# A two-layer decoder trunk on one core: where the head's weights land, the order of the normalisation between the layers, and 7 weight with 5 landing buffers

## The chip, the core and the metric

The kernel runs on one core of a Trainium2 chip. The metric is the device time of one execution in microseconds (us), less is better; several runs are taken and their median is compared.

## What is computed

Two layers, a sequence of 256 tokens, 2048 features, all in float32. Each layer projects its input x into queries, keys, values and gates of two attention branches (12 heads of 128 each), runs a dilated sliding-window attention and a forgetting attention, projects both up, merges them with gates computed from x, projects once more, and normalises:

```python
def hybrid_layer(x, pos, w_in, b_forget, b_gate, w_up_a, w_up_b, w_out, ln_g, ln_b):
    h = jnp.einsum('bsd,dc->bsc', x, w_in)
...
    return layer_norm(alpha * x + y, ln_g, ln_b)

def layer_norm(x, g, b):
    x32 = x.astype(jnp.float32)
    mu = jnp.mean(x32, axis=-1, keepdims=True)
    var = jnp.mean(jnp.square(x32 - mu), axis=-1, keepdims=True)
    y = (x32 - mu) * lax.rsqrt(var + LN_EPS)
    return (y * g.astype(jnp.float32) + b.astype(jnp.float32)).astype(x.dtype)
```

Nearly all of the work is the products of x, and of what comes from it, with the weights: 357 MB of weights are read once.

## The kernel before, in words

**Two halves of a number.** Every operand of a product is kept as a high half (ACT's copy into the fp32r type) and a low half (source less high half, on DVE); `split` (L68 to L70) makes both. A product of a weight tile of 128 x 128 with x is one 512-column matmul, the weight's high half with both halves of x (L164), and one 256-column matmul, its low half with x's high half (L162).

**Pieces.** The weights come in 716 pieces. `Piece.prep` loads one into a landing buffer `raw` (L63 to L66, on SP's queue, 7 buffers) and splits it into a weight buffer `w` (L82, 6 buffers), from which `Piece.run` feeds PE. A large piece is 128 x 1024: eight k-tiles (128 rows) of one unit, a unit being 128 columns of one projection. When a unit is complete, `fold` adds the two halves of its PSUM tile: ACT copies one (`c`, L173) and DVE adds the other (`p`, L175).

**The first units of a layer.** The first four units (`SIDE`) of each layer don't run one after the other. Their pieces are interleaved, and PE goes by pairs of k-tiles through all four: such a pair of one unit is called a block below (two 512-column and two 256-column matmuls, 1536 columns), 32 blocks in all. So PE can begin when the first tile of x is there. In layer 0 these units are cut into five chunks each, of 2, 2, 4, 4 and 4 k-tiles (20 pieces); in layer 1 into two of eight (8 pieces). x lives in eight tiles of two k-tiles each, here x_81 to x_88 by the names of the program; in layer 0 they are loaded by `load_x` (L114 to L120) into idle slots of the pool `s2` (L59), between the pieces, and split. x_81's load goes out on SP's queue, x_82's on ACT's, the others on SP's. Eight matmuls on zeros (`keep_warm`, L136 to L140) run ahead of the first real one.

**Between the layers.** `ln_stats` (L533 to L553) gets the mean and the reciprocal deviation from the sums that PE made, spreads them over the partitions by PE (`pm`, `pa`), and subtracts the mean from the first tile (DVE) and from the second (POOL). `ln_next` (L568 to L591) then makes x_81 to x_88 again, tile by tile: a front (subtract the mean, L565; multiply, L562 or L566; the affine step and x's high half on ACT, L577 for the first two tiles, L579 and L584 for the others; for the first two tiles the affine step on DVE too, L582) and a back (x's low half, DVE L589). The main loop (L655 on) lists fronts and backs in the order front 0, back 0, front 1, front 2, back 1, front 3, back 2 and so on, holds each behind the one before by `tc.issue_after`, and calls `prep_to` for the pieces. The framework's scheduler decides the rest of each engine's order: where splits of pieces stand between these steps.

Of the kernel before, what the change touches and what calls it, by code (L numbers as in the profile page):

```python
# [42 lines left out]
def trunk(ctx: ExitStack, tc: tile.TileContext, xt, w_st, w_v, w_vf, w_up, w_o,  # L43
# [17 lines left out]


    def load_raw(ap, n):  # L63
        t = wp.tile([128, SLOT], F32, name="raw", tag="raw", bufs=7)
        nc.sync.dma_start(t[:, :n], ap)
        return t[:, :n]  # L66

# [4 lines left out]
    class Piece:  # L72


        def __init__(self, unit, ap, kts, w):
            self.unit, self.ap, self.kts, self.w = unit, ap, kts, w
            self.first = self.last = False

        def prep(self):
            n = len(self.kts) * self.w  # L80
            raw = load_raw(self.ap, n)
            t = wp.tile([128, 2 * W_PART + 64], F32R, name="w", tag="w", bufs=6)  # L82
            o = W_OFF if self.w == 128 else V_OFF
            self.t = t[:, o:o + 2 * W_PART].rearrange("p (a b) -> p a b", a=2)
            split(self.t[:, 0, :n], self.t[:, 1, :n], raw)
# [28 lines left out]
    def load_x(k0, n):  # L114
        for k in range(k0, k0 + n, 2):
            raw = slot("xraw")
            (nc.scalar if k == 2 else nc.sync).dma_start(raw, xt[:, k:k + 2, :])
            x = xs[k // 2]
            for i in ((slice(0, 1), slice(1, 2)) if k == 0 else (slice(0, 2),)):
                split(x[:, i, 0], x[:, i, 1], raw[:, i])  # L120
# [81 lines left out]
    def build_layer(l):  # L202
# [97 lines left out]
        def mixer_pair(br, p):  # L300
# [77 lines left out]
            if br == 0 and p == 0:  # L378
                us = [q_u[0], k_u[0], z_u[0], q_u[1], k_u[1], v_unit, z_u[1]]
                chunks = (2, 2, 4, 4, 4) if l == 0 else (8, 8)  # L380
                for u in us[:SIDE]:
                    u.cut(chunks)
            elif has_f:
                us = [v_unit] + q_u + k_u + z_u
            else:
                us = q_u + k_u + [v_unit] + z_u
# [146 lines left out]
        def ln_stats():  # L533
            pst = ln["pst"]
            mu, m, rs = (sm.tile([128, 2], F32, name=n, tag=n, bufs=2) for n in ("mu", "m", "rs"))
            nc.vector.tensor_scalar(mu, pst[:, 0], 1.0 / D, None, op0=ALU.mult)
            nc.scalar.activation(m, pst[:, 0], AF.Square, scale=1.0 / D)
            nc.vector.scalar_tensor_tensor(m, pst[:, 1], 1.0 / D, m, op0=ALU.mult, op1=ALU.subtract)
            pm = spread(mu, "pm")
            if not final:  # L540
                keep_warm(3)
            nc.scalar.activation(m, m, AF.Sqrt, bias=eps)
            nc.vector.reciprocal(rs, m)
            pa = spread(rs, "pa")
            if not final:
                keep_warm(6)
            ms = att.tile([128, S], F32, name="ms", tag="lnc", bufs=1)
            nc.scalar.activation(ms, pm, AF.Copy)
            for i in range(2):
                nc.vector.tensor_tensor(ln[0][:, i], ln[0][:, i], pm, op=ALU.subtract)  # L550
            for j2 in pooled:
                nc.gpsimd.tensor_tensor(ln[j2], ln[j2], both(ms), op=ALU.subtract)
            ln["pm"], ln["pa"] = pm, pa  # L553

        def affine(j2):
            return ([t[:, l * KT + 2 * j2 + i:l * KT + 2 * j2 + i + 1] for i in range(2)] for t in (lng, lnb))

        def centred(j2):
            r = ln[j2]
            if j2 == 0:  # L560
                for i in range(2):
                    ins = nc.vector.tensor_tensor(r[:, i], r[:, i], ln["pa"], op=ALU.mult)  # L562
                return ins
            if j2 not in pooled:
                nc.vector.tensor_tensor(r, r, both(ln["pm"]), op=ALU.subtract)  # L565
            return nc.vector.tensor_tensor(r, r, both(ln["pa"]), op=ALU.mult)  # L566

        def ln_next(j2, quick):  # L568

            r, x = ln[j2], xs[j2]  # L570
            g, b = affine(j2)

            def front():
                ins = centred(j2)
                for i in range(2):
                    if quick:
                        nc.scalar.activation(x[:, i, 0], r[:, i], AF.Identity, scale=g[i], bias=b[i])  # L577
                    else:
                        nc.scalar.activation(r[:, i], r[:, i], AF.Identity, scale=g[i], bias=b[i])  # L579
                if quick:  # L580
                    for i in range(2):
                        ins = nc.vector.tensor_scalar(r[:, i], r[:, i], g[i], b[i], op0=ALU.mult, op1=ALU.add)  # L582
                else:
                    nc.scalar.activation(x[:, :, 0], r, AF.Copy)  # L584
                return ins

            def back():
                for i in (range(2) if quick else (slice(0, 2),)):
                    ins = nc.vector.tensor_tensor(x[:, i, 1], r[:, i], x[:, i, 0].bitcast(F32), op=ALU.subtract)  # L589
                return ins  # L590
            return front, back  # L591

        def ln_last(j2):
            r = ln[j2]
# [62 lines left out]
    for g in order:  # L657
        done += len(g)
        n = number[id(g[0].unit)]
        if g[0].first and n in norms:  # L660

            stats, apply = norms[n]
            stats()
            stages = [apply(j2, j2 < 2) for j2 in range(KT // 2)]
            run = [stages[0][0], stages[0][1], stages[1][0]]
            for j2 in range(2, KT // 2):
                run += [stages[j2][0], stages[j2 - 1][1]]
            run.append(stages[-1][1])
            ins = None
            for i, f in enumerate(run):  # L670
                if i == 9:
                    with tc.issue_after(ins.ins):
                        prep_to(done + 2)
                if ins is None:
                    ins = f()
                else:
                    with tc.issue_after(ins.ins):
                        ins = f()
        prep_to(done + 4)
        for p in g:  # L680
            if p.first:
                for f in jobs.get(number[id(p.unit)], []):
                    f()
                if p.unit.before:
                    p.unit.before()
        if len(g) > 1:
            for i in range(0, len(g[0].kts), 2):
                for p in g:
                    for part in range(2):
                        p.run(i, part)  # L690
                        p.run(i + 1, part)
        else:

            for part in range(2):
                for i in range(len(g[0].kts)):
                    g[0].run(i, part)
        for p in g:
            if p.last and p.unit.after:
                p.unit.after()
# [87 lines left out]
```

## Time and profile before

| | us |
|---|---|
| runs | 1979.55, 1979.7, 1981.81 |
| median | 1979.7 |
| profiled execution | 1979.52 |
| its span in the trace | 1977.7 |

The profile is that of one execution. Times in it count from the start of the span. PE is TensorE, PEld its weight loads, DVE VectorE, ACT ScalarE, POOL GpSimd, SP the engine that issues most transfers; a name with q is an engine's queue. A row of a timeline groups like instructions that follow one another: start, length of the group, what it is, how many, and in brackets how long the engine had idled before it and for whom. The matmuls' ends are modelled, so the spacing of starts tells more than the lengths.

### The profile page before, as it was taken

The page shows a single profiled execution, that of the slowest core. Times are in us where ns is not written, and L with a number is a line of the kernel's source. Part 1 is how long each engine was busy: PE and PEld are TensorE (multiplying, and loading weights), DVE is VectorE, ACT ScalarE, POOL GpSimd, SP SyncE. Part 2 cuts the span into 40 slices and gives each one's busy share as a digit, 9 for nine tenths or more (in the row PEclk, how much of TensorE's full clock was granted, in tenths as well). Part 3 has the DMA queues.
Part 4 walks back from the last instruction along what each step waited for, and adds up shares of the span by engine and source line. Part 5 has one row for each costly group of instructions (what it writes and reads, how often), then busy time and mean ns, then how long its engine had stood idle before and what let it go on. Part 6 is the DMA issues. An engine that isn't in the chain of part 4 may idle for free.

```text
span 1977.7 us, 29731 instructions
## 1 busy us (share of the span) xinstructions
PE 1957.8 (99%) x11449; PEld 1727.2 (87%) x11449; DVE 1269.8 (64%) x1908; ACT 987.3 (50%) x1558; POOL 69.5 (4%) x64
## 2 busy tenths in 40 slices
PE   9999999999999999999999999999999999999997
PEld 7888888889888888888888888888898888888886
DVE  7666665555555555668787666655555555556686
ACT  6444444444544445555465444445454444445544
POOL 0000000001000000001100000000010000000022
PEclk9999999999999999999999999999999999999998
DMA  9655555666656556665555555556666665556651
GB/s 307 204 180 179 172 169 172 192 197 211 185 178 183 179 170 180 183 202 192 160 181 171 179 176 178 166 181 185 203 203 185 185 179 179 170 174 191 210 184 64
DMA packets 108630, 362.74 MB, mean 183 GB/s; under 512 B 12464, under 2 KB 15944, under 8 KB 108488
## 3 DMA queue, kind: packets, MB, share of 16 engines
q1 hardware_dynamic: 107320, 357.42, 58.5%
q0 software_dynamic: 1024, 3.17, 0.7%
q8 instruction: 89, 1.46, 0.3%
q14 instruction: 53, 0.43, 0.1%
q10 hardware_dynamic: 144, 0.26, 0.1%
HBM read 358.68 MB, written 2.12 MB: 182 GB/s over the span
## 4 chain that ended last, share of the span: by engine, by line
PE 98%; DVE 1%; DMA 0%; ACT 0%; issue 0%; DVEq 0%; ACTq 0%
PE mm L164 53%; PE mm L162 27%; PE mm L353 8%; PE mm L355 4%; PE ps_s L258 1%; PE po L287 1%; PE pt L278 1%; PE po L288 1%; PE ps_s L257 1%; PE mm L351 0%; PE mm L348 0%; PE mm L349 0%; DMA xraw<-xt 0%; DVE gated L566 0%; DMA raw<-w_st 0%
## 5 line engine op out<-in xcount | busy, mean ns | idle before, releaser
L70 DVE TENSOR_TENSOR w<-raw,w 128x1024 fp32r<-128x1024 f32 (+3 forms) x716 | 840.5, 1178 | 443.5 <-ACT w L69 442.1
L69 ACT ACTIVATE w<-raw 128x1024 fp32r<-128x1024 f32 (+3 forms) x716 | 717.9, 1004 | 455.5 <-issue 222.6
L164 PE MATMUL mm<-x,w 128*128 128x512 f32 x3328 | 851.2, 396 | 6.4 <-DVE x L589 3.1
L164 PEld LDWEIGHTS mm<-x,w 128*128 128x128 f32 x3328 | 594.3, 188 | 109.9 <-ACT x L577 2.7
L162 PEld LDWEIGHTS mm<-x,w 128*128 128x128 f32 x3328 | 454.0, 188 | 39.2 <-DVE w L70 1.4
L162 PE MATMUL mm<-x,w 128*128 128x256 f32 x3328 | 463.8, 279 | 0.0
L173 ACT ACTIVATE c<-mm 128x256 f32<-128x256 f32 x320 | 120.3, 384 | 456.2 <-PE mm L162 422.5
L175 DVE TENSOR_TENSOR p<-mm,c 128x256 f32<-128x256 f32 x252 | 106.8, 425 | 186.9 <-ACT c L173 186.4
L164 PE MATMUL mm<-gated,w 128*128 128x512 f32 x768 | 196.6, 391 | 0.0
L353 PE MATMUL mm<-w,x 128*128 128x512 f32 x704 | 176.7, 393 | 0.0
L164 PEld LDWEIGHTS mm<-gated,w 128*128 128x128 f32 x768 | 135.3, 188 | 21.1
L353 PEld LDWEIGHTS mm<-w,x 128*128 128x128 f32 x704 | 126.1, 188 | 22.7
L164 PE MATMUL mm<-merged,w 128*128 128x512 f32 x480 | 120.1, 392 | 0.0
L162 PEld LDWEIGHTS mm<-gated,w 128*128 128x128 f32 x768 | 108.3, 188 | 10.4
L162 PE MATMUL mm<-gated,w 128*128 128x256 f32 x768 | 111.2, 279 | 0.0
L355 PEld LDWEIGHTS mm<-w,x 128*128 128x128 f32 x704 | 94.7, 188 | 7.4
L164 PEld LDWEIGHTS mm<-merged,w 128*128 128x128 f32 x480 | 86.0, 188 | 15.5 <-DVE merged L70 0.5
L355 PE MATMUL mm<-w,x 128*128 128x256 f32 x704 | 96.5, 279 | 0.0
L162 PEld LDWEIGHTS mm<-merged,w 128*128 128x128 f32 x512 | 68.1, 188 | 4.8
L162 PE MATMUL mm<-merged,w 128*128 128x256 f32 x512 | 69.9, 279 | 0.0
L447 POOL TENSOR_TENSOR u<-x 128x512 f32<-128x512 f32 x16 | 31.7, 1982 | 603.9 <-DVE merged L70 242.4
L267 ACT ACTIVATE z<-z,s 128x128 f32<-128x128 f32 x96 | 42.3, 444 | 0.0
(128 smaller groups left out, 910.9 us busy)
## 6 DMA issues: line engine op xcount, KB each, us to landing
raw<-w_st SPq DMA_DIRECT2D x408, 512.0 KB, 3.9
raw<-w_up SPq DMA_DIRECT2D x128, 384.0 KB, 3.1
raw<-w_v SPq DMA_DIRECT2D x88, 512.0 KB, 4.4
raw<-w_o SPq DMA_DIRECT2D x64, 512.0 KB, 4.1
raw<-w_vf SPq DMA_DIRECT2D x8, 536.0 KB, 4.4
raw<-w_st SPq DMA_DIRECT2D x12, 256.0 KB, 5.6
nb<-cum POOLq DMA_DIRECT2D x12, 256.0 KB, 4.5
yt<-gated SPq DMA_DIRECT2D x8, 256.0 KB, 2.1
```

The lines of the kernel that those rows point to most:

```text
L69: nc.scalar.activation(hi, src, AF.Copy)
L70: nc.vector.tensor_tensor(lo, src, hi.bitcast(F32), op=ALU.subtract)
L162: nc.tensor.matmul(o, w[:, 1], a[:, 0], start=False, stop=last)
L164: nc.tensor.matmul(ps(), w[:, 0], a, start=first, stop=False)
L173: nc.scalar.activation(c, ps[:, S:], AF.Copy, scale=scale)
L175: nc.vector.tensor_tensor(dst, ps[:, :S], c, op=ALU.add)
L257: nc.tensor.matmul(ps[:, 0], q[:, :128], k[:, :128], start=True, stop=True)
L258: nc.tensor.matmul(ps[:, 1:3].rearrange("p a b -> p (a b)"), q[:, 128:], k, start=True, stop=True)
L267: nc.scalar.activation(z[:, sl], z[:, sl], AF.Exp, scale=-1.0, bias=s4[:, c:c + 1], accum_out=s4[:, 2 + c:3 + c])
L353: nc.tensor.matmul(o, xh, w, start=first, stop=False)
L355: nc.tensor.matmul(o[:, :NV], xl, w[:, 0], start=False, stop=last)
L447: nc.gpsimd.tensor_tensor(u, x[:, :, 0], x[:, :, 1], op=ALU.add)
```

## The change

- The landing buffers go from 7 to 5 and the weight buffers from 6 to 7.
- The 20 pieces of the first four units of layer 0 land in slots of `s2` (`wraw`) instead of `raw`. x_82 is loaded by SP's queue like the rest.
- In `ln_stats` between the layers, 12 warm matmuls are asked for behind `pa` instead of 6.
- In `ln_next`, the subtraction of the mean is a step of its own (`shift`); for the first two tiles DVE writes its affine result to a new slot `y`; before, it overwrote `r`, which ACT reads too.
- The order becomes front 0, back 0, front 1, shift 2, back 1, front 2, then for each tile shift, front and the back of the tile before. One piece is asked for ahead of the statistics; two more calls for pieces stand behind the steps of tiles 4 and 5, in place of one.

```diff
@@ -61,7 +61,7 @@
 
 
     def load_raw(ap, n):
-        t = wp.tile([128, SLOT], F32, name="raw", tag="raw", bufs=7)
+        t = wp.tile([128, SLOT], F32, name="raw", tag="raw", bufs=5)
         nc.sync.dma_start(t[:, :n], ap)
         return t[:, :n]
 
@@ -74,12 +74,16 @@
 
         def __init__(self, unit, ap, kts, w):
             self.unit, self.ap, self.kts, self.w = unit, ap, kts, w
-            self.first = self.last = False
+            self.first = self.last = self.head = False
 
         def prep(self):
             n = len(self.kts) * self.w
-            raw = load_raw(self.ap, n)
-            t = wp.tile([128, 2 * W_PART + 64], F32R, name="w", tag="w", bufs=6)
+            if self.head:
+                raw = slot("wraw", (128, 2 * S))[:, :n]
+                nc.sync.dma_start(raw, self.ap)
+            else:
+                raw = load_raw(self.ap, n)
+            t = wp.tile([128, 2 * W_PART + 64], F32R, name="w", tag="w", bufs=7)
             o = W_OFF if self.w == 128 else V_OFF
             self.t = t[:, o:o + 2 * W_PART].rearrange("p (a b) -> p a b", a=2)
             split(self.t[:, 0, :n], self.t[:, 1, :n], raw)
@@ -114,7 +118,7 @@
     def load_x(k0, n):
         for k in range(k0, k0 + n, 2):
             raw = slot("xraw")
-            (nc.scalar if k == 2 else nc.sync).dma_start(raw, xt[:, k:k + 2, :])
+            nc.sync.dma_start(raw, xt[:, k:k + 2, :])
             x = xs[k // 2]
             for i in ((slice(0, 1), slice(1, 2)) if k == 0 else (slice(0, 2),)):
                 split(x[:, i, 0], x[:, i, 1], raw[:, i])
@@ -380,6 +384,9 @@
                 chunks = (2, 2, 4, 4, 4) if l == 0 else (8, 8)
                 for u in us[:SIDE]:
                     u.cut(chunks)
+                    for piece in u.pieces:
+
+                        piece.head = l == 0
             elif has_f:
                 us = [v_unit] + q_u + k_u + z_u
             else:
@@ -543,7 +550,7 @@
             nc.vector.reciprocal(rs, m)
             pa = spread(rs, "pa")
             if not final:
-                keep_warm(6)
+                keep_warm(12)
             ms = att.tile([128, S], F32, name="ms", tag="lnc", bufs=1)
             nc.scalar.activation(ms, pm, AF.Copy)
             for i in range(2):
@@ -561,7 +568,7 @@
                 for i in range(2):
                     ins = nc.vector.tensor_tensor(r[:, i], r[:, i], ln["pa"], op=ALU.mult)
                 return ins
-            if j2 not in pooled:
+            if final and j2 not in pooled:
                 nc.vector.tensor_tensor(r, r, both(ln["pm"]), op=ALU.subtract)
             return nc.vector.tensor_tensor(r, r, both(ln["pa"]), op=ALU.mult)
 
@@ -569,6 +576,10 @@
 
             r, x = ln[j2], xs[j2]
             g, b = affine(j2)
+            y = slot("y") if quick else r
+
+            def shift():
+                return nc.vector.tensor_tensor(r, r, both(ln["pm"]), op=ALU.subtract)
 
             def front():
                 ins = centred(j2)
@@ -579,16 +590,16 @@
                         nc.scalar.activation(r[:, i], r[:, i], AF.Identity, scale=g[i], bias=b[i])
                 if quick:
                     for i in range(2):
-                        ins = nc.vector.tensor_scalar(r[:, i], r[:, i], g[i], b[i], op0=ALU.mult, op1=ALU.add)
+                        ins = nc.vector.tensor_scalar(y[:, i], r[:, i], g[i], b[i], op0=ALU.mult, op1=ALU.add)
                 else:
                     nc.scalar.activation(x[:, :, 0], r, AF.Copy)
                 return ins
 
             def back():
                 for i in (range(2) if quick else (slice(0, 2),)):
-                    ins = nc.vector.tensor_tensor(x[:, i, 1], r[:, i], x[:, i, 0].bitcast(F32), op=ALU.subtract)
+                    ins = nc.vector.tensor_tensor(x[:, i, 1], y[:, i], x[:, i, 0].bitcast(F32), op=ALU.subtract)
                 return ins
-            return front, back
+            return shift, front, back
 
         def ln_last(j2):
             r = ln[j2]
@@ -660,22 +671,19 @@
         if g[0].first and n in norms:
 
             stats, apply = norms[n]
+            prep_to(done + 1)
             stats()
-            stages = [apply(j2, j2 < 2) for j2 in range(KT // 2)]
-            run = [stages[0][0], stages[0][1], stages[1][0]]
-            for j2 in range(2, KT // 2):
-                run += [stages[j2][0], stages[j2 - 1][1]]
-            run.append(stages[-1][1])
-            ins = None
-            for i, f in enumerate(run):
-                if i == 9:
-                    with tc.issue_after(ins.ins):
-                        prep_to(done + 2)
-                if ins is None:
-                    ins = f()
-                else:
-                    with tc.issue_after(ins.ins):
-                        ins = f()
+            shift, front, back = zip(*(apply(j2, j2 < 2) for j2 in range(KT // 2)))
+            run = [front[0], back[0], front[1], shift[2], back[1], front[2]]
+            for j2 in range(3, KT // 2):
+                run += [shift[j2], front[j2], back[j2 - 1]]
+                if j2 in (4, 5):
+                    run.append(lambda n=j2 - 1: prep_to(done + n))
+            run.append(back[-1])
+            ins = run[0]()
+            for f in run[1:]:
+                with tc.issue_after(ins.ins):
+                    ins = f() or ins
         prep_to(done + 4)
         for p in g:
             if p.first:
```

How the rows of the two programs stand where it moves them. **SP at the head**: the order in which the loads are issued (xraw for x, raw or wraw for weights), before:

```order
L117 DMA xraw<-xt 128x512
L65 DMA raw<-w_st 128x256 x7
L117 DMA xraw<-xt 128x512 x2
L65 DMA raw<-w_st 128x256
L65 DMA raw<-w_st 128x512 x4
L117 DMA xraw<-xt 128x512
L65 DMA raw<-w_st 128x512 x4
L117 DMA xraw<-xt 128x512 x2
L65 DMA raw<-w_st 128x512 x4
L117 DMA xraw<-xt 128x512
L65 DMA raw<-w_st 128x1024
```

and with the change:

```order
L121 DMA xraw<-xt 128x512
L83 DMA wraw<-w_st 128x256 x4
L121 DMA xraw<-xt 128x512
L83 DMA wraw<-w_st 128x256 x4
L121 DMA xraw<-xt 128x512
L83 DMA wraw<-w_st 128x512 x4
L121 DMA xraw<-xt 128x512 x2
L83 DMA wraw<-w_st 128x512 x4
L121 DMA xraw<-xt 128x512 x2
L83 DMA wraw<-w_st 128x512 x4
L121 DMA xraw<-xt 128x512
L65 DMA raw<-w_st 128x1024
```

x_82 now comes fifth behind x_81 on the same queue, the second group of four pieces stays together, and each pair of x tiles keeps its place among the pieces.

**ACT between the layers**, from x_85's high half on (L69 is the high half of a piece, L173 the copy `c` of the first units' sums, x_85 to x_88 the high halves of x), before:

```order
L584 ACTIVATE x_85<-gated 128x2x256
L69 ACTIVATE w<-raw 128x1024 x2
L579 ACTIVATE gated<-gated,lnb,lng 128x256 x2
L69 ACTIVATE w<-raw 128x1024
L584 ACTIVATE x_86<-gated 128x2x256
L69 ACTIVATE w<-raw 128x1024
L579 ACTIVATE gated<-gated,lnb,lng 128x256 x2
L584 ACTIVATE x_87<-gated 128x2x256
L579 ACTIVATE gated<-gated,lnb,lng 128x256 x2
L584 ACTIVATE x_88<-gated 128x2x256
L69 ACTIVATE w<-raw 128x1024 x2
L173 ACTIVATE c<-mm 128x256 x3
```

and with the change:

```order
L595 ACTIVATE x_85<-gated 128x2x256
L69 ACTIVATE w<-raw 128x1024 x3
L590 ACTIVATE gated<-gated,lnb,lng 128x256 x2
L69 ACTIVATE w<-raw 128x1024
L595 ACTIVATE x_86<-gated 128x2x256
L590 ACTIVATE gated<-gated,lnb,lng 128x256 x2
L595 ACTIVATE x_87<-gated 128x2x256
L590 ACTIVATE gated<-gated,lnb,lng 128x256 x2
L595 ACTIVATE x_88<-gated 128x2x256
L69 ACTIVATE w<-raw 128x1024
L177 ACTIVATE c<-mm 128x256 x3
L69 ACTIVATE w<-raw 128x1024
```

Three splits instead of two follow x_85, one instead of two stands between x_86 and x_87, and one instead of two stands ahead of the three copies `c`.

**DVE in the same stretch**, from the multiplication of x_86's tile on (L70 is the low half of a piece, L175 the sum `p`), before:

```order
L566 TENSOR_TENSOR gated<-gated,pa 128x512
L589 TENSOR_TENSOR x_86<-gated,x_86 128x2x256
L565 TENSOR_TENSOR gated<-gated,pm 128x512
L70 TENSOR_TENSOR w<-raw,w 128x1024
L566 TENSOR_TENSOR gated<-gated,pa 128x512
L589 TENSOR_TENSOR x_87<-gated,x_87 128x2x256
L70 TENSOR_TENSOR w<-raw,w 128x1024 x2
L589 TENSOR_TENSOR x_88<-gated,x_88 128x2x256
L70 TENSOR_TENSOR w<-raw,w 128x1024 x2
L175 TENSOR_TENSOR p<-mm,c 128x256 x3
```

and with the change:

```order
L573 TENSOR_TENSOR gated<-gated,pa 128x512
L600 TENSOR_TENSOR x_86<-gated,x_86 128x2x256
L582 TENSOR_TENSOR gated<-gated,pm 128x512
L70 TENSOR_TENSOR w<-raw,w 128x1024
L573 TENSOR_TENSOR gated<-gated,pa 128x512
L600 TENSOR_TENSOR x_87<-gated,x_87 128x2x256
L70 TENSOR_TENSOR w<-raw,w 128x1024
L600 TENSOR_TENSOR x_88<-gated,x_88 128x2x256
L70 TENSOR_TENSOR w<-raw,w 128x1024
L179 TENSOR_TENSOR p<-mm,c 128x256 x4
```

One split instead of two stands ahead of the first sums, which follow one another without a split between the third and the fourth. PE's order is the same but for the six warm matmuls and one pair of 256-column matmuls; 264 instead of 62 of its instructions wait for more than one engine.

## Rows read from the trace of the kernel before

**Rows 1.** The page: busy time of each engine; the chain that ended last

```profile
PE 1957.8 (99%) x11449; PEld 1727.2 (87%) x11449; DVE 1269.8 (64%) x1908; ACT 987.3 (50%) x1558; POOL 69.5 (4%) x64
...
PE 98%; DVE 1%; DMA 0%; ACT 0%; issue 0%; DVEq 0%; ACTq 0%
```

**Rows 2.** Busy time by stretch; us, busy of each engine (count), clock, DMA share, GB/s

```profile
29.83:979.00 949.17, 949.17 (x5566) 838.71 (x5565) 611.01 (x908) 472.65 (x740) 30.74 (x27) 1.00 0.61 188
...
986.37:1011.20 24.83, 24.15 (x128) 20.75 (x128) 21.13 (x31) 16.91 (x26) 0.00 (x0) 0.93 0.40 124
...
1013.25:1960.00 946.75, 946.75 (x5543) 836.34 (x5544) 603.01 (x900) 465.39 (x731) 31.14 (x27) 1.00 0.59 179
```

**Rows 3.** Timeline of the head: start, length, engine, line, work, count [idle before <-releaser]

```profile
0.74 0.40 ACTq L117 DMA_DIRECT2D xraw<-xt  x1
...
1.46 3.50 PE L139 MATMUL pw<-warm 128*128 128x512 f32 x8 [1.46 <-DVE warm L133]
...
5.20 0.72 ACT L69 ACTIVATE x<-xraw 128x256 fp32r<-128x256 f32 x2 [2.75 <-DMA xraw<-xt]
...
6.29 0.97 PE L164 MATMUL mm<-x,w 128*128 128x512 f32 x3 [1.33 <-ACT w L69]
...
9.66 3.60 SPq L65 DMA_DIRECT2D raw<-w_st  x4
...
14.28 0.63 ACT L69 ACTIVATE w<-raw 128x512 fp32r<-128x512 f32 x1 [0.54 <-DMA raw<-w_st]
```

**Rows 4.** Timeline of the head, PE alone

```profile
11.24 0.63 PE L164 MATMUL mm<-x,w 128*128 128x512 f32 x2
...
16.03 0.62 PE L164 MATMUL mm<-x,w 128*128 128x512 f32 x2
...
16.72 0.62 PE L164 MATMUL mm<-x,w 128*128 128x512 f32 x2
```

**Rows 5.** The page: DMA queues; packets, MB, share of 16 engines

```profile
q10 hardware_dynamic: 144, 0.26, 0.1%
```

**Rows 6.** Busy time by stretch, the first microseconds

```profile
0.00:1.50 1.50, 0.04 (x1) 0.04 (x1) 0.58 (x3) 0.33 (x1) 0.20 (x4) 1.00 0.00 0
...
4.00:5.20 1.20, 0.96 (x3) 0.42 (x2) 0.00 (x0) 0.00 (x0) 0.00 (x0) 1.00 1.02 337
```

**Rows 7.** Timeline after the head, DVE alone

```profile
38.25 1.22 DVE L70 TENSOR_TENSOR w<-raw,w 128x1024 fp32r<-128x1024 f32 x1
```

**Rows 8.** Timeline between the layers, PE alone

```profile
983.45 0.47 PE L139 MATMUL pw<-warm 128*128 128x512 f32 x1
...
986.37 0.94 PE L164 MATMUL mm<-x,w 128*128 128x512 f32 x3 [2.45 <-DVE x L589]
...
1002.50 0.73 PE L164 MATMUL mm<-x,w 128*128 128x512 f32 x2 [0.68 <-DVE x L589]
...
1013.25 0.93 PE L164 MATMUL mm<-x,w 128*128 128x512 f32 x3 [1.88 <-DVE p L175]
```

**Rows 9.** Timeline between the layers, DVE alone

```profile
984.99 0.91 DVE L582 TENSOR_SCALAR gated<-gated,lng,lnb 128x256 f32<-128x256 f32 x2 [0.34 <-ACT x L577]
...
1001.75 0.69 DVE L589 TENSOR_TENSOR x<-gated,x 128x512 fp32r<-128x512 f32 x1 [0.66 <-ACT x L584]
...
1010.41 2.36 DVE L70 TENSOR_TENSOR w<-raw,w 128x1024 fp32r<-128x1024 f32 x2 [2.16 <-ACT w L69]
...
1012.69 1.08 DVE L175 TENSOR_TENSOR p<-mm,c 128x256 f32<-128x256 f32 x3
```

**Rows 10.** Timeline between the layers, ACT alone

```profile
1009.32 2.01 ACT L69 ACTIVATE w<-raw 128x1024 fp32r<-128x1024 f32 x2 [2.75 <-PE mm L162]
...
1011.24 0.91 ACT L173 ACTIVATE c<-mm 128x256 f32<-128x256 f32 x3
```

**Rows 11.** The page: DMA issues; operation, count, KB each, median us to landing

```profile
raw<-w_v SPq DMA_DIRECT2D x88, 512.0 KB, 4.4
```

**Rows 12.** One line's instructions, L287: count, ns least/median/most, first to last start

```profile
L287 PEldq EVENT_SEMAPHORE  x24: 51/51/51, 68.3 to 1731.5; - x24
```

## Prediction

> **What bounds the kernel now.** I read the shares first: PE is busy for 1957.8 of 1977.7 us, and the chain of waits is PE for 98% [rows 1]. In the table of busy time by stretch PE is then full through the first layer, 949.17 of 949.17 us [rows 2], and the second, its like, differs in nothing here. There is nothing to win there, only something to lose. What is left is the head (to 29.83), the stretch between the layers (979 to 1013.25) and the tail, whose orders are alike in both kernels. The change can win in the first two alone.
>
> **The head.** x_81 is split from 5.20, when the first xraw has landed; the first product starts at 6.29, 1.09 later [rows 3]. The work then goes in blocks: one pair of k-tiles of one of the four units, 0.69 us (from 16.03 to 16.72 [rows 4]), 32 blocks in all. Twenty of them follow one another from 16.03 to 29.83 (20 x 0.69 = 13.80). Before that, five blocks stretch from 11.24 to 16.03, 4.79 us where 3.45 would do: 1.34 us lost [rows 4]. There ACT stands idle for landings of raw (0.54 before 14.28 is one), and the loads that feed it were issued late: from 9.66 on, four issues on SP take 3.60 us where one issue by itself takes 0.40 [rows 3]. With seven landing buffers a load must wait until DVE has finished the piece seven before it.
>
> Part 1, x on one queue. x_82's 256 KB go out at 0.74 on ACT's queue beside x_81's on SP's [rows 3]; that one transfer is all of queue q10, and it lands 4.2 after its issue, near 4.95 [rows 5]. Now it stands behind x_81 and four pieces on SP. At the 337 GB/s of 4.00 to 5.20 [rows 6], 262 KB are 0.78 us, so I let x_81 land 0.78 earlier, at 4.4, and the first product start at 5.51. Bounds: nothing gained (6.29) and the end of the warm products, 1.46 + 3.50 = 4.96 [rows 3]. I take the middle one, since all 16 engines together move what they move, whoever comes first. x_82 is needed on chip four blocks after the start, less 1.3 for its two splits, near 5.51 + 2.76 - 1.3 = 7.0; four pieces of 128 KB and x_82 behind x_81 are 0.79 MB, 2.3 us at 337 GB/s, so it lands by 6.7 at the latest. The extra issue on SP is 0.4 us [rows 3], hidden by the same margin.
>
> Part 2, the first twenty pieces land in idle slots. No load of the head waits for a buffer, so the queue stays full. By bytes at 337 GB/s, pieces 8 to 11 land at about 8.6, 9.3, 10.1 and 10.9, and PE wants them split at 11.0, 11.7, 12.4 and 13.1; a split of this form costs 0.63 on ACT [rows 3] and about as much on DVE. The 1.34 us go. Late next is the fifth large piece after the head, whose lo half DVE starts at 38.25 [rows 7], ending 1.22 later at 39.47; PE wants it at 29.83 + 4 x 2.75 = 40.83 (a large piece is eight k-tiles of one unit, four blocks, 2.75 us). Everything moves earlier together, but one rotary product of 0.61 now stands ahead of it: the margin falls from 1.4 to 0.8 and nothing stalls. Head: 0.78 + 1.34 = **2.12 us less**. Its poor end is 0.8 less (x_81 as late as now and the 0.54 wait stays), its good end 2.67 less (first product at 4.96).
>
> **Between the layers.** PE waits 2.45 us for x_81's lo half, starts at 986.37, waits 0.68 before 1002.50 for x_86, ends the block work at 1011.2 and starts again only at 1013.25, after DVE's sum p [rows 8]. The clock of this stretch averages 0.93 over 24.83 us [rows 2], that is 3.5 us at half speed (1.2 instead of 2.4 GHz) just after the 2.45 us idle, a loss of 1.7. The twelve blocks from 1002.50 to 1011.2 take 8.7, of which 8.3 is block work: what sets the end is when x_86 comes, so I cost the clock's recovery at nothing; DVE, busy 21.13 of 24.83 [rows 2], is its cover.
>
> Part 3, the start. The affine op of DVE waits 0.34 for ACT, since ACT still reads the tile that it overwrites [rows 9]. With its own tile y the wait goes and x_81 comes 0.3 earlier. The six added warm products run while PE idles: the one of now ends at 983.92 [rows 8], and by a block's 0.69 for 1536 columns each takes 0.23, so they end near 985.3, ahead of x_81 near 986.0. At 0.44 each (3.50 for eight [rows 3]) they would end at 986.6 and cost 0.6 there, hidden by the wait for x_86.
>
> Part 4, x_86. Before it DVE does two splits, the three steps of x_85, a shift, a split and the front; then it waits 0.66 for ACT, which has a split ahead of the copy [rows 9]. Now the shift of a tile comes before the front of the next, and the same splits are spread differently. Adding durations along both engines, with 0.60 for a 512-wide step (0.72 if it hangs on the one before), 1.13 a split on DVE, 1.0 on ACT, I get x_86's end at 1002.16 in place of 1002.5: 0.34 earlier. The block work ends at about 1002.16 + 8.3 + 0.1 = 1010.6.
>
> Part 5, the end. Two splits that ACT begins at 1009.32 (2.01 us), after waiting 2.75 for PE to give back weight buffers, stand ahead of the copy c at 1011.24; the lo halves on DVE (1010.41, 2.36) stand ahead of p at 1012.69 [rows 9, 10]. With seven weight buffers one of them is done before, and only one stands there: ACT 1008.7 to 1009.7, DVE to 1010.9. Then c at 1010.6, 0.4 long, p at 1010.95 to 1011.0, and PE 0.56 after p's start as now: 1011.5 in place of 1013.25. Boundary: **1.75 us less**. Its poor end is 0.3 less (x_86 alone comes earlier, two splits stand ahead of the sums as now), its good end 2.0 less (x_86's whole wait of 0.68 goes).
>
> **Buffers.** Five landing buffers: a load of 512 KB lands in 4.4 us [rows 11], and a buffer is wanted again five pieces (13.75 us) later, less some 2.2 for the splits. Costed at nothing in the layers; if that cover went, PE would idle there. Between the layers the fifth load is issued near 995, when DVE has split a piece, lands near 999 and is wanted at 999.6.
>
> **Sum.** The profiled execution took 1979.52, the span of 1977.7 and 1.8 around it, 0.2 under the median of 1979.7. 1979.52 - 2.12 - 1.75 = **1975.6**. A measurement of this kernel tells about 0.2% from no change, that is 3.96 us: faster begins at 1975.74, hardly above the forecast.
>
> **Rivals.** *x_81 has the engines to itself, 1975.1, chance 0.16.* The two x transfers landed near 4.95 and 5.2 [rows 3, 5] although one had seven loads behind it on its queue, as if the queues took turns. Then x_81 alone needs half of the time from 1.5, before which nothing moves [rows 6], to 5.2, lands near 3.4, and the warm products at 4.96 are the floor: the head gives 2.67. The Trainium skill ("DMA: Bandwidth & Descriptors", Queues, rings and completion order) says that each DMA engine takes turns between the queue rows, a packet at a time; by it this rival would hold, and no row here shows the packets.
>
> *The head gives less, 1977.0, chance 0.09.* x_81 lands no sooner and a landing wait of 0.54 stays. For it: the four pieces behind x_81 stay on its queue, and bytes already move at 337 GB/s before 5.2 [rows 6]. 1979.52 - 0.8 - 1.75.
>
> *The boundary gives only 0.3, 1977.1, chance 0.15.* The hand-made chain is off by a split: ACT takes x_86's copy after one more split, or two stand before the sums. 1979.52 - 2.12 - 0.3.
>
> *Slower: waits on TensorE's queue, 1986.0, chance 0.08.* With other buffer numbers 202 more of PE's instructions wait for two engines at once, which makes a queue instruction of its own; such a one takes 51 ns [rows 12]. If none were hidden, 202 x 0.051 = 10.3 us would come on top of the forecast. It decides from 39 ns each, (3.9 + 3.96) / 202. Against it: 62 of them stand in the kernel now, such as the 24 of line 287 [rows 12], and PE is full in the stretches that hold them [rows 2].
>
> **How the numbers follow.** The forecast, both places as summed, has 0.52: 1974.3 to 1976.6. Of the rivals 0.16, 0.09, 0.15 and 0.08. Faster: the first rival and two thirds of the forecast's chance, 0.50. Slower: the waits, 0.08. Same: the rest, 0.42. The range goes from 1974.3 (both good ends, 1974.85, and 0.55 of the clock's 1.7 that I costed at nothing) to 1978.4 (both poor ends: 0.8 and 0.3 less).
>
> **What would show it.** First product at 5.5 or sooner, blocks of 0.69 from there and their end near 27.7; y's affine op without a wait; no half-speed stretch after x_81, or one that changes nothing; x_86 near 1002.2 less the head's 2.1; one split ahead of c; PE idle about 1 us before the sums instead of 1.9. The prediction is wrong if PE shows idle time inside the layers, if blocks still stretch behind landings, or if x_83 to x_86 hold PE longer than 0.7 us each.

## The result and the profile after

The changed kernel takes 1996.98 us (median of 4 runs, 1996.73 to 1997.24) against 1979.62: a ratio of 1.0084, 95% interval 1.0071 to 1.0096. It is slower, by 17.4 us, and outside the forecast range. The profiled execution took 1997.24, its span 1995.5.

Where did it go? PE's starts in the trace cut the span into five stretches and the tail. First the changed kernel, busy time by stretch (length, busy time and count of PE, PEld, DVE, ACT, POOL, then clock, DMA share, GB/s):

```profile
0.00:29.99 29.99, 28.03 (x137) 23.14 (x137) 19.16 (x35) 19.34 (x34) 0.20 (x4) 1.00 0.91 310
29.99:988.85 958.86, 958.56 (x5566) 845.90 (x5565) 611.94 (x908) 474.21 (x742) 31.26 (x27) 1.00 0.60 185
988.85:995.54 6.69, 6.33 (x41) 5.25 (x40) 3.77 (x13) 3.00 (x6) 1.29 (x1) 1.00 0.05 20
995.54:1021.33 25.79, 23.55 (x129) 19.84 (x129) 22.04 (x33) 17.83 (x30) 0.00 (x0) 1.00 0.39 123
1021.33:1979.92 958.59, 958.59 (x5565) 845.98 (x5565) 602.86 (x900) 466.30 (x733) 30.90 (x27) 1.00 0.58 178
```

The same cuts of the kernel before (the first layer is in [rows 2]):

```profile
0.00:29.83 29.83, 26.96 (x136) 21.89 (x137) 18.94 (x35) 19.16 (x35) 0.20 (x4) 1.00 0.91 311
...
979.00:986.37 7.37, 4.93 (x35) 4.22 (x34) 4.05 (x13) 3.10 (x7) 1.27 (x1) 1.00 0.08 31
986.37:1013.25 26.88, 24.32 (x128) 20.78 (x129) 23.18 (x34) 18.96 (x31) 0.00 (x0) 0.94 0.40 124
1013.25:1962.41 949.16, 949.16 (x5564) 838.75 (x5565) 603.18 (x900) 465.93 (x732) 31.14 (x27) 1.00 0.58 179
```

| stretch | before | after | difference | predicted |
|---|---|---|---|---|
| head | 29.83 | 29.99 | +0.16 | -2.12 |
| layer 0 | 949.17 | 958.86 | +9.69 | 0 |
| between the layers | 34.25 | 32.48 | -1.77 | -1.75 |
| layer 1 | 949.16 | 958.59 | +9.43 | 0 |
| tail (rest of the span) | 15.29 | 15.58 | +0.29 | 0 |

The loss is in the layers, in both alike, and there PE is full: the same number of matmuls, busy to the last 0.3 us, takes 1% longer. So PE waits for no other engine there; the single matmul has grown. These are rows of the page, with the mean ns of one behind the busy time. The 256-column products of the changed kernel:

```profile
L166 PEld LDWEIGHTS mm<-x,w 128*128 128x128 f32 x3328 | 460.9, 190 | 38.0 <-DVE w L70 0.8
L166 PE MATMUL mm<-x,w 128*128 128x256 f32 x3328 | 471.9, 282 | 0.0
```

And of the kernel before:

```profile
L162 PEld LDWEIGHTS mm<-x,w 128*128 128x128 f32 x3328 | 454.0, 188 | 39.2 <-DVE w L70 1.4
L162 PE MATMUL mm<-x,w 128*128 128x256 f32 x3328 | 463.8, 279 | 0.0
```

From the starts of the single matmuls, a piece of sixteen (eight 512-column products, then eight 256-column ones) takes 2818 ns on average instead of 2789, and a layer has some 330 times sixteen such products: 9.5 us. Most of it is in the 256-column products, spaced 119.1 ns instead of 116.4. It makes no difference whether the matmul behind has a wait of its own on the queue (the last product of a piece takes 120 ns with and without).

### The profile page after: what moved, and what is told of

Read it like the earlier page. It is cut to its first block, busy times and chain, and to the rows that moved or that the text cites. A ratio compares the mean times of both kernels' runs of the same rounds, so it can differ in the third digit from the quotient of the medians.

```text
span 1995.5 us, 29661 instructions
## 1 busy us (share of the span) xinstructions
PE 1978.3 (99%) x11455; PEld 1742.9 (87%) x11455; DVE 1269.2 (64%) x1908; ACT 988.1 (50%) x1558; POOL 69.8 (3%) x64
## 3 DMA queue, kind: packets, MB, share of 16 engines
HBM read 358.68 MB, written 2.12 MB: 181 GB/s over the span
## 4 chain that ended last, share of the span: by engine, by line
PE 97%; DVE 1%; DMA 1%; ACT 0%; issue 0%; SPq 0%; DVEq 0%; ACTq 0%
PE mm L168 52%; PE mm L166 27%; PE mm L357 8%; PE mm L359 4%; PE po L291 1%; PE ps_s L262 1%; PE pt L282 1%; PE ps_s L261 1%; PE po L292 1%; PE mm L355 0%; PE mm L353 0%; PE mm L352 0%; DVE gated L573 0%; DMA xraw<-xt 0%; DVE w L70 0%; DMA wraw<-w_st 0%
## 5 line engine op out<-in xcount | busy, mean ns | idle before, releaser
L70 DVE TENSOR_TENSOR w<-raw,w 128x1024 fp32r<-128x1024 f32 (+2 forms) x696 | 828.9, 1194 | 452.9 <-ACT w L69 451.4
L69 ACT ACTIVATE w<-raw 128x1024 fp32r<-128x1024 f32 (+2 forms) x696 | 708.1, 1019 | 463.1 <-issue 225.5
L166 PE MATMUL mm<-x,w 128*128 128x256 f32 x3328 | 471.9, 282 | 0.0
L166 PEld LDWEIGHTS mm<-gated,w 128*128 128x128 f32 x768 | 109.0, 190 | 10.6
```

What stands on the lines that cost most here:

```text
L69: nc.scalar.activation(hi, src, AF.Copy)
L70: nc.vector.tensor_tensor(lo, src, hi.bitcast(F32), op=ALU.subtract)
L166: nc.tensor.matmul(o, w[:, 1], a[:, 0], start=False, stop=last)
```

## The experiments

**What makes every matmul longer.** Nothing in PE's order explains it, so I looked at where the operands lie in memory. The profile has no addresses; what follows is worked out from the sizes of the tiles and the order in which the framework lays them out. The buffers of a pool are laid out by first use. Before, the head's loads used `raw` first: 7 x 4288 bytes from 26560 on, then the weights at 56576, a multiple of 256. With the change the head lands in `s2`, so the weight buffers come first, at 26560, which is 192 above a multiple of 256; and 7 x 8960 + 5 x 4288 bytes are 384 more than 6 x 8960 + 7 x 4288, so x and all behind it moved by 128 modulo 256. With W_OFF's 48 floats, the weights of most pieces begin at 192 modulo 256 before and at 128 after, x at 0 before and at 128 after. So the distance from x to the weights, modulo 256, went from 192 to 0. Four runs tell the two places apart, and the waits from both.

First the weights alone moved back, in the changed kernel:

```diff
-W_OFF = 48
-V_OFF = 16
+W_OFF = 0
+V_OFF = 32
```

> The changed kernel with the weights put elsewhere inside their buffers (W_OFF 48 to 0, V_OFF 16 to 32), so that they begin at the same address modulo 256 bytes as in the kernel before; x and all other tiles stay where the change put them. Both layers lost 9.6 us each (958.9 and 958.6 against 949.2), with PE full and most matmuls a few ns longer. Theory 1, the weights' place in memory makes them longer: 1996.98 - 19.1 = about 1977.9, a layer 949.2. Theory 2, the place of x and what comes from it: 1997, a layer 958.7. Theory 3, the 202 added waits on TensorE's queue: 1997. Theory 4, the distance between weights and x modulo 256 bytes (0 in the changed kernel, 192 before, 64 here): anything between, since 64 was not seen before.

Measured: 1984.59 (ratio to the kernel before 1.0021, 1.0012 to 1.003), layers 952.5 and 952.2. Two thirds of the loss went, not all: neither theory 1 nor 2 by itself.

Then x alone moved back (`SLOT` to `SLOT + 32` in `load_raw`'s tile, bufs=5):

> The changed kernel with each landing buffer 128 bytes longer, so that x and everything behind it begins at the same address modulo 256 bytes as in the kernel before (0); the weights stay where the change put them (128 modulo 256). Theory 1 (place of the weights): 1997, a layer 958.7. Theory 2 (place of x): about 1977.9, a layer 949.2. Theory 3 (queue waits): 1997. Theory 4 (distance, 128 here): something else than in the run with the weights moved.

Measured: 2004.89 (1.0123, 1.0108 to 1.0138), layers 962.5 and 962.3: worse than the change itself. Theory 2 falls.

Both moved back (`SLOT + 16`, and `eps` made 64 bytes longer, ahead of the weights):

> The changed kernel with 64 bytes ahead of the weights and 64 more in each landing buffer, so that weights (192) and x (0) both begin at the same address modulo 256 bytes as before. Theories 1, 2 and 4 all: a layer 949.2, and 1996.98 - 19.1 = about 1977.9, 1.7 less than before, because the stretch between the layers took 1.78 less (32.47 against 34.25) and the head 0.16 more. Theory 3 (202 queue waits, all kept here): 1997.

Measured: 1978.68 (0.999, 0.998 to 0.9999), layers 950.0 and 949.4. The whole loss is gone with all queue waits kept, so theory 3 falls.

And the kernel before with its weights put at 128 modulo 256, nothing else:

```diff
-W_OFF = 48
-V_OFF = 16
+W_OFF = 32
+V_OFF = 0
```

> The kernel before, with the weights put where the change has them modulo 256 bytes (W_OFF 48 to 32, V_OFF 16 to 0), and nothing else. Theory 1 (place of the weights): 1979.6 + 19.1 = about 1998.7, a layer 958.8. Theories 2 and 3: 1979.6, a layer 949.2. Theory 4 (distance, 128 here): as in the run where x was moved back.

Measured: 2007.09 (1.0136, 1.012 to 1.0153), layers 962.2 and 962.3. Two constants cost the old kernel 1.4%. It agrees with the run with x moved back (the distance is 128 in both): within the pieces, behind the first product, the 512-column products are spaced 232.8 ns and the 256-column ones 118.8 in either. That points to the distance; the two share their places as well, so the next run keeps the distance and has neither place:

```diff
-W_OFF = 48
-V_OFF = 16
+W_OFF = 32
+V_OFF = 0
```

(in the changed kernel)

> The changed kernel with W_OFF 48 to 32 and V_OFF 16 to 0 and nothing else: weights at 64 and x at 128 modulo 256 bytes, neither where it was before, but the distance between them (192) as before. If the distance counts: a layer 949.4, a 512-column matmul every 229.3 ns in a piece, total about 1978.5, as with both moved back. If the place of each counts by itself: a pair not seen yet, a layer between 952 and 962, as in the other runs with x at 128 or weights not at 192, total above 1983.

Measured: 1978.81 (0.9989, 0.998 to 0.9998). Its layers by stretch:

```profile
30.09:979.61 949.52, 949.21 (x5567) 838.68 (x5565) 611.39 (x908) 473.84 (x742) 30.55 (x27) 1.00 0.61 187
...
1012.09:1961.39 949.30, 949.30 (x5565) 838.79 (x5566) 603.36 (x900) 466.00 (x733) 30.64 (x27) 1.00 0.58 180
```

The distance counts:

| run | weights, x modulo 256 | distance | layer 0, layer 1 |
|---|---|---|---|
| before | 192, 0 | 192 | 949.2, 949.2 |
| change | 128, 128 | 0 | 958.9, 958.6 |
| weights back | 192, 128 | 64 | 952.5, 952.2 |
| x back | 128, 0 | 128 | 962.5, 962.3 |
| before, weights moved | 128, 0 | 128 | 962.2, 962.3 |
| both back | 192, 0 | 192 | 950.0, 949.4 |
| same distance | 64, 128 | 192 | 949.5, 949.3 |

A single piece shows the same: the first six pieces behind the attention's scores take 2975 ns in all three runs at 192, 2989 at 0, 2970 at 64 and 3003 with x back. The distance is between weights and x and everything that lies behind x. That 256 is the right modulus is not shown: the runs tell 0, 64, 128 and 192 apart, and a longer period was not tried.

Is 192 the best? One run with sixteen places in turn:

```diff
-            o = W_OFF if self.w == 128 else V_OFF
+            o = 4 * (Piece.count % 16)
+            Piece.count += 1
```

> The version with both moved back, but each piece of weights is put 16 bytes further into its buffer than the piece before, sixteen places in turn, so that one run shows every distance to x from 0 to 240 bytes modulo 256 in steps of 16. If the distance counts: pieces at 0, 64, 128 and 192 show the spacings of the four runs so far (512 columns: 230.9, 232.4, 232.7, 229.3 ns; 256 columns: 134.5, 130.9, 134.1, 132.5 ns by the mean over all), and the others lie on a smooth or stepped line between. If it is the place of the whole buffer or another tile instead: all sixteen alike. The total is the mean of the sixteen, 1978 to 2005.

Measured: 2000.03, one run. The pieces at 192 look worst: up to 470 us, six of seven take 2962 to 2972 ns. But these six lie right behind the attention's scores, and the same six take 2975 in the kernel before, their first product 420 ns there as here. With sixteen places in turn, a place falls on the same spot of PE's order again and again, so the run can't rank the places. At 240 six pieces took 2748 to 2785 ns, the least on average (2783 for the same six in the kernel before). The place that looked best, for all pieces:

```diff
-W_OFF = 48
-V_OFF = 16
+W_OFF = 60
+V_OFF = 28
```

(in the version with both moved back)

> The version with both moved back, with W_OFF 48 to 60 and V_OFF 16 to 28: all weights stand 240 (v: 112) bytes from x modulo 256, the place whose pieces were shortest in the run with sixteen places (2759.6 and 2761.4 ns a piece of sixteen matmuls, against 2790.8 and 2780.6 at 192 and 64 in the kernel before). If a piece's own place sets its length: 29 ns of some 2790 less, a layer near 940, total near 1959. If the rhythm also hangs on the piece before it (in that run a piece at 192 took 2949, not 2791): no telling, a layer anywhere between 942 and 965.

Measured: 1987.57 (1.0033, 1.002 to 1.0045), layers 954.0 and 953.7: a miss of the first theory. The six pieces that took 2748 to 2785 in the sweep all take 2785 now, at the same place. So something besides a piece's own distance counts, and what was not found. Of the five distances tried for all pieces, 192 is the shortest; others weren't tried.

**The head.** In the changed kernel, PE's timeline, then ACT's at the first four pieces of 256 KB:

```profile
5.04 1.48 PE L168 MATMUL mm<-x,w 128*128 128x512 f32 x3
...
12.48 0.63 PE L168 MATMUL mm<-x,w 128*128 128x512 f32 x2
...
13.48 0.73 PE L168 MATMUL mm<-x,w 128*128 128x512 f32 x2
...
14.55 0.64 PE L168 MATMUL mm<-x,w 128*128 128x512 f32 x2
...
15.95 0.73 PE L168 MATMUL mm<-x,w 128*128 128x512 f32 x2 [0.36 <-DVE x L70]
...
16.75 0.63 PE L168 MATMUL mm<-x,w 128*128 128x512 f32 x2
```

```profile
10.23 0.64 ACT L69 ACTIVATE w<-wraw 128x512 fp32r<-128x512 f32 x1
11.23 0.63 ACT L69 ACTIVATE w<-wraw 128x512 fp32r<-128x512 f32 x1 [0.37 <-DMA wraw<-w_st]
12.79 0.63 ACT L69 ACTIVATE w<-wraw 128x512 fp32r<-128x512 f32 x1 [0.93 <-DMA wraw<-w_st]
13.68 0.63 ACT L69 ACTIVATE w<-wraw 128x512 fp32r<-128x512 f32 x1 [0.25 <-DMA wraw<-w_st]
```

x_81 came early: ACT splits it from 3.53. But the first three products take 1.48 instead of 0.97 [rows 3], spaced 427 ns, and three blocks from 12.48 to 15.95 take 3.47 instead of 2.07: 1.4 lost, as before (1.34, [rows 4]). The slow first products are a matter of the clock: the trace's records of the granted clock begin, at full speed, at 7.33 us here and at 4.49 in the kernel before, and a row counts time without a record as 1.00. From 7.48 on the same products come every 230 ns. The head doesn't hang on that: with both moved back the records begin at 4.65, and the head still ends at 30.13.

The blocks wait for landings. An issue of SP waits until the load eight before it has landed (piece 8's goes out at 6.35, when that one landed at 6.34). Either these eight loads in flight or the transfers themselves are the limit.

x_82 on ACT's queue again (`load_x` as before, both moved back):

> The version with both moved back, with x_82 on ACT's queue again as in the kernel before. The head ended at 30.0 in the changed kernel (29.4 to 30.3 in the runs with moved tiles) against 29.83 before: x_81 landed at 3.7 instead of 5.2, but blocks still waited for landings. Theory 1, the loads of SP's queue are held by eight in flight (each issue follows the landing of the eighth before it): a transfer outside of the eight brings the later pieces 0.4 to 0.8 sooner, head 29.3 to 29.7, though x_81 lands near 5.2. Theory 2, the transfers themselves are the limit: head 29.8 to 30.3, total as with both moved back, 1978.3 to 1978.7.

Measured: 1978.66 (0.9988, 0.9978 to 0.9997), head 29.67: theory 1's range, but the eight profiles that have the changed order of the head and seven weight buffers, the changed kernel's included, spread from 29.38 to 31.21, so it shows nothing.

The head's pieces in the five landing buffers (`piece.head = False`):

> The version with both moved back, with the head's pieces in the five landing buffers instead of idle slots. Theory 1 and 2 of the head (eight in flight, or the transfers) say that the slots bring nothing against seven landing buffers; with five, a load waits for DVE five pieces before it, so if the buffers bind at all it is here: head 30.2 to 33, and the layers as they were. If idle slots are what keeps the queue full: head over 32.

Measured: 1980.75 (0.9998, 0.9989 to 1.0008), head 31.43, only just outside that spread. But the loads move 242 GB/s in the first 24 us (row below) instead of 281 to 314 in the eight runs with the changed order and slots, and the 16 DMA engines are busy for 0.75 of it instead of 0.88 to 0.91. Five buffers do bind; the slots are what makes five enough.

Every second unit's pieces on POOL's queue:

```diff
-                nc.sync.dma_start(raw, self.ap)
+                (nc.gpsimd if self.unit.odd else nc.sync).dma_start(raw, self.ap)
```

> The changed kernel with the weights' distance as before (the fix of two offsets), with the head's pieces of every second unit loaded by POOL's queue instead of SP's, x all on SP's. Theory 1 of the head (eight in flight on SP's queue hold it): twice as many may be under way, blocks stop waiting for landings, head 27.3 to 28.6, total 1976 to 1977.5. Theory 2 (the transfers themselves): head 29.4 to 30.5, total as without it, 1978.8.

Measured: 1982.49 (1.0008, 0.9998 to 1.0017), head 34.48: worse than either theory had it. Some 1.7 us of that is PE at half clock, by the trace from 16.21 to 19.62, after it had idled 1.66. The first 24 us, in the kernel before, the changed kernel, with five landing buffers, and with two queues:

```profile
0.00:24.00 24.00, 21.13 (x102) 16.76 (x103) 15.69 (x31) 16.05 (x30) 0.20 (x4) 1.00 0.90 298
```

```profile
0.00:24.00 24.00, 22.04 (x102) 17.90 (x103) 16.36 (x31) 16.70 (x30) 0.20 (x4) 1.00 0.91 301
```

```profile
0.00:24.00 24.00, 20.50 (x95) 16.23 (x96) 13.39 (x27) 13.95 (x26) 0.20 (x4) 1.00 0.75 242
```

```profile
0.00:24.00 24.00, 19.39 (x81) 15.18 (x82) 13.26 (x27) 14.03 (x28) 5.72 (x14) 0.93 0.89 303
```

And 6 to 16 us alone, where the blocks stretch, in the changed kernel and with two queues:

```profile
6.00:16.00 10.00, 9.50 (x48) 7.35 (x46) 7.05 (x14) 7.12 (x14) 0.00 (x0) 1.00 1.00 317
```

```profile
6.00:16.00 10.00, 6.97 (x36) 5.24 (x35) 4.75 (x11) 4.24 (x10) 1.40 (x3) 1.00 1.00 343
```

The last columns are the answer. Over 24 us it is 298, 301 and 303 GB/s; from 6 to 16 us the DMA engines are busy all the time in both (share 1.00), and the second queue brings 343 instead of 317. The eight runs with one queue spread from 281 to 314 over 24 us and from 297 to 333 from 6 to 16, so little of this stands out. With more loads under way each takes longer: the 256 KB pieces of SP's queue land 10.6 us after their issue (median) instead of 5.9. So hardly more bytes arrive, they arrive in another order, and PE waits (1.23 before 9.90 and 1.66 before 15.01). The transfers limit the head, and too few buffers make it worse (242). Why they bring 317 here and 404 from 16 to 20 us isn't shown. The Trainium skill ("DMA: Bandwidth & Descriptors", Issuing engines are not separate DMA queues) says that transfers issued from several engines run on the same 16 DMA engines and save only time of issue. The two-queue run agrees over 24 us, with its 303 against 301.

**Between the layers.** The changed kernel, PE's timeline, then ACT's and DVE's:

```profile
993.31 1.87 PE L143 MATMUL pw<-warm 128*128 128x512 f32 x7
995.54 0.74 PE L168 MATMUL mm<-x,w 128*128 128x512 f32 x2 [0.36 <-DVE x L600]
...
1011.81 0.74 PE L168 MATMUL mm<-x,w 128*128 128x512 f32 x2 [1.00 <-DVE x L600]
...
1021.33 0.93 PE L168 MATMUL mm<-x,w 128*128 128x512 f32 x3 [0.74 <-DVE p L179]
```

```profile
1018.53 1.06 ACT L69 ACTIVATE w<-raw 128x1024 fp32r<-128x1024 f32 x1 [2.65 <-PE mm L166]
1019.50 0.92 ACT L177 ACTIVATE c<-mm 128x256 f32<-128x256 f32 x3
```

```profile
1019.62 1.23 DVE L70 TENSOR_TENSOR w<-raw,w 128x1024 fp32r<-128x1024 f32 x1 [3.02 <-ACT w L69]
1020.76 1.41 DVE L179 TENSOR_TENSOR p<-mm,c 128x256 f32<-128x256 f32 x4
```

One split instead of two stands ahead of c and p, as forecast, and PE's wait there is 0.74 instead of 1.88 [rows 8]. The clock is 1.00 throughout, where it was 0.94. x_86 is waited for longer, 1.00 instead of 0.68, since PE gets there sooner. Two runs take the parts apart.

Six warm products again (`keep_warm(12)` to `keep_warm(6)`, weights at the old distance):

> The changed kernel with the weights' distance as before, and 6 instead of 12 warm products asked for between the layers, as in the kernel before. The stretch took 32.47 with the change and 34.25 before, where PE ran at half speed for 3.4 us after 2.45 us idle. My prediction's theory (DVE sets the pace, the warm products buy nothing): 32.5 to 32.8. Rival: the half-speed stretch comes back and costs its 1.7, 33.5 to 34.2.

Measured: 1978.88 (0.9991, 0.9982 to 1.0), the stretch 33.28: halfway. Its busy time by stretch and PE's timeline:

```profile
986.87:1012.40 25.53, 24.14 (x127) 20.87 (x128) 21.08 (x31) 16.68 (x28) 0.00 (x0) 0.93 0.40 124
```

```profile
986.87 0.97 PE L168 MATMUL mm<-x,w 128*128 128x512 f32 x3 [1.76 <-DVE x L600]
...
1003.95 0.74 PE L168 MATMUL mm<-x,w 128*128 128x512 f32 x2 [1.39 <-DVE x L600]
```

After 1.76 us idle the half-speed stretch is back (0.93), and x_86 comes later too: PE, slower, gives the weight buffers back later, and the splits that wait for them stand ahead of x_86's steps on DVE and ACT. So the warm products are worth 33.28 - 32.48 = 0.80 (32.48 holds at the old distance too), and PE's waits for x hide the rest of the 1.7.

Six weight and seven landing buffers again, all else as changed, both at their old places:

> The version with both moved back, with 6 weight and 7 landing buffers as in the kernel before, and all else of the change. The prediction's theory (the seventh weight buffer takes one split from ahead of the first sums): two splits stand there again, PE's wait before it goes on is 2.1 instead of 1.03, the stretch 33.6. Rival (the order of the steps did it): 32.5. The head with 7 landing buffers and slots: 30.0, as with 5. Added waits on PE's queue gone: the layers 949.2 to 949.4 either way if they cost nothing.

Measured: 1980.62 (1.0, 0.9991 to 1.0009), the stretch 33.65, layers 949.2 and 949.3, head 29.93. ACT and PE:

```profile
1008.80 2.01 ACT L69 ACTIVATE w<-raw 128x1024 fp32r<-128x1024 f32 x2 [2.63 <-PE mm L166]
1010.72 0.91 ACT L177 ACTIVATE c<-mm 128x256 f32<-128x256 f32 x3
```

```profile
1012.74 1.62 PE L168 MATMUL mm<-x,w 128*128 128x512 f32 x6 [1.91 <-DVE p L179]
```

Two splits stand ahead again and PE waits 1.91. The buffer numbers are worth 33.65 - 32.48 = 1.17. Both were changed back at once; that it is the seventh weight buffer is read from ACT's wait, which is for PE to give one back. PE's queue has 63 event instructions here and 267 with the added waits, and the layers are the same (949.2 and 949.3; 949.5 and 949.3 at the same distance with the waits): they cost nothing.

## Why the prediction was wrong

- **Buffers, "costed at nothing in the layers": the step that failed.** I asked whether five landing buffers keep up, and they do: PE idles 0.3 us in the first layer and none in the second. What I didn't ask is where the tiles lie once the buffers are other in number and first use. The distance between weights and x went from 192 to 0 modulo 256 bytes, and each layer took 9.6 us more, 19.1 in all. With the distance put back the change is worth 2.4 us (1978.81 against 1981.21, compared side by side), less than the 3.96 of my bound and than the 3.87 of the forecast.
- **Head, 2.12 less: wrong, 0.16 more.** Part 1's step was right in kind, and the rival with x_81 alone on the engines was nearer: split from 3.53 (rival 3.4, forecast 4.4), first product at 5.04 (4.96 and 5.51). It bought nothing, since the blocks wait for later landings anyway. The step that failed is part 2's, "no load of the head waits for a buffer, so the queue stays full", and the landings "by bytes at 337 GB/s": pieces 8 to 11 were to land at 8.6, 9.3, 10.1 and 10.9, and by the trace they landed at 10.1, 11.1, 12.7 and 13.6. I took the 3.60 for four issues for waits on buffers, but with no buffer to wait for, four such issues take 3.60 again. And 337 GB/s is the rate of 4.00 to 5.20; from 6 to 16 us it is 302 in the kernel before and 317 with the change.
- **Between the layers, 1.75 less: 1.77, in part by luck.** Part 5's step is right: PE's wait before the sums fell by 1.14 (forecast 1.15), and the run with the old buffer numbers gives 1.17 back. Part 3 was mis-sized: the first product comes 0.68 earlier, not 0.3 (7.37 to 6.69); y's wait is gone as forecast, and its two steps take 0.73 instead of 0.91. Part 4's 0.34 didn't come from the order of the steps: counted from the end of the layer, x_86's block starts at 23.50 before, at 23.78 with six warm products and at 22.96 with twelve. So "the clock's recovery at nothing" was wrong by 0.80, and that made up for part 4. From the first product to the end of the block work, waits for x included, it is 25.0 us in both kernels.
- **The rival that ended on the other side** named the waits on TensorE's queue. The side was right and the cause was not: the layers take the same time with those waits as without.

## What to carry to other kernels

Where TensorE is full, look at its matmuls' spacing before and after any change of buffers, even of their number or first use: in this kernel an operand's place in memory, relative to the other's, cost a per cent with PE waiting for nothing. Put the distance back first (here two constants), and only then judge the change. Where a head waits for landings, look at the bytes per microsecond first: here a second queue hardly raised them, and the head grew.

The version to keep is the changed kernel with W_OFF = 32 and V_OFF = 0: 1978.81, faster than the kernel before (0.9989, 0.998 to 0.9998) and 18 us faster than the change as made.

## What I had not expected of the hardware

- The time of a matmul hangs on the distance of its operands modulo 256 bytes: at 192, 240, 64, 0 and 128 a layer takes 949.3, 953.8, 952.4, 958.7 and 962.3 us, with the same instructions. Why isn't settled. Which of TensorE's reads meet each other wasn't tried, and a piece's own distance isn't all: six pieces at 240 took 2748 to 2785 ns among other places, and 2785 when all lie at 240.
- Right behind the attention's scores, the second product of a piece starts 420 ns after the first, and the piece takes 2975 ns, where pieces between others take some 2760 in the kernel before. A test of places has to compare the same pieces.
- A row's granted clock of 1.00 at the start of the span can mean that there is no record yet. In the changed kernel PE works from 1.46 on and the records begin at 7.33 us; the eight warm products (3.78 us for all) and the first real ones, 427 ns each from 5.04 on, ran at about half the later pace, 230 ns. In the seven other runs with the same head order and seven weight buffers, the records begin between 4.36 and 7.57. What decides when isn't shown.
